# Hybrid attention and RWKV-7 layer: the preparation of head pairs in three chains with tiles of their own

## The chip, the core and the metric

The kernel runs on one core of a Trainium2 chip. The metric is the device time of one execution in microseconds (us). A core has five engines with a queue each: TensorE (PE; its weight loads are listed as PEld), VectorE (DVE), ScalarE (ACT), GpSimd (POOL) and SyncE (SP), which here issues all DMA transfers. Each engine takes its instructions in the order in which they were written and waits on semaphores for the others.

## The reference

One decoder layer for 1024 tokens of width 1024, in float32:

```
u = rmsnorm(x);  z = u @ w_in                       # 1024 x 6048
o_attn = dilated attention over z[:, :2304]         # 3 groups (dilation 1, 4, 16) of 4 heads of 64
o_rwkv = rwkv7 time mix over z[:, 2304:4000]        # 8 heads of 64; state S = S*w + sa b' + v k'
merged = sigmoid(z_g1)*(o_attn @ w_attn_up) + sigmoid(z_g2)*(o_rwkv @ w_rwkv_up)
h = x + rmsnorm(merged @ w_out)
h = h + rmsnorm(square(relu(rmsnorm(h) @ w_ff_in)) @ w_ff_out)      # 4096 wide
h = h + rmsnorm((p @ w_ple) * sigmoid(h @ w_ple_gate))
```

The delta-rule recurrence of the time mix runs over the tokens; everything else is products and elementwise work.

## The kernel before

All wide products are made of three fp32r products each (high by high, low by high, high by low parts; helper mm3, lines 203, 205 and 207). One such product, 128x128 by 128x512, is called a dense product here. A 128-column tile of w_in against the 1024 tokens ("z") takes 48 of them, in two halves of 24. There are 48 such tiles: 2 for the small decay and gate factors, 12 for RWKV (r, k, v of four pairs of heads), 18 for attention (q, k, v of six units) and 16 for the two gates, whose z is only written to DRAM (gscr). Then come the merge (8 tiles, products named bk and z), w_out, the wide MLP and the gated embedding.

RWKV works on pairs of heads, w = 0 to 3. For each pair: `elementwise(w)` makes the decays (Ep, En), the normalised keys (kk), and the tiles AR and BK, and from their products A the triangular matrices TM; `invert(w)` inverts 32 matrices by 31 steps of two small DVE operations each (pt and X), puts the halves together by transposes and the products tq and tr, into TN; `fold(w)` makes the values UV (products vt, kv), the transposed BK (bt) and the folded TM (fq); `scan(w)` runs 16 chunks of 64 tokens, each a product q with the state S, an addition on DVE into UV, two products y, and the new state S on DVE; `post` normalises four chunks at a time (yq, sq, vc, yt, oc) and stores them. Then attention runs six units one after another (scores sc, softmax, transposes pt, products po), `natural` and `combine` mix the three groups (rw, cb), and the merge follows.

The order on PE is set by a planner (class Order, lines 70 to 156), which runs when the program is built: it keeps a list of chains (Python generators with a priority), lets the first chain that is due emit its next instructions, and otherwise emits one dense product from the first tile whose gate is open. A chain says by its yields how long it has to wait by the planner's own costs. The order of the other engines is made by the scheduling layer below. Which z tiles may be emitted when is said by gates: those of RWKV wait for the tiles r, k and v of the pair before; those of attention by `attn_ok` (line 745); those of the gates are always open. When nothing is left, a chain's instructions stand in the program without dense products between them.

The chain `rwkv` (line 732) prepares pair 0 (elementwise, then invert), and then for each pair folds it, spawns the preparation of the next pair and scans. Mp, X, pt and TQ of an inversion lie in the tiles a, kk, En and Ep of the elementwise part, TN in BT; BK has one tile for all pairs; yq of a scan lies in px. Attention's q and k of units 0 and 1 use the tiles r, k, Ep, En, a and kk, and so their gate waits for the last inversion, `("T", NU - 1)`.

Of the kernel before, what the change touches and what calls it, by code (L numbers as in the profile page):

```python
# [159 lines left out]
def layer(ctx: ExitStack, tc: tile.TileContext, x, pT, wz, wup, w_out, wff1, w_ff2, w_ple, w_pleg,  # L160
# [54 lines left out]
    def wait(cond):  # L215
        while not cond():
            yield 0.1
# [41 lines left out]
    with tc.tile_pool(name="xin", bufs=1) as xp:  # L259
# [75 lines left out]
        for q in range(4):  # L335
# [143 lines left out]
    c3 = lambda t: t.rearrange("p (c t) -> p c t", c=NCH)  # L479
    U = {}  # L480

    def elementwise(w):
# [86 lines left out]
    def invert(w):  # L569
        TA = U[w]["TM"][:, :, :, 0:64].rearrange("p h c t -> p (h c) t")  # L570
        Mp = rtile([64, 32, 32], "Mp", "a")
        X = rtile([64, 32, 32], "X", "kk")
        pt = rtile([64, 1024], "pt", "En")
        G.memset(X, 0.0)
        G.memset(X.rearrange("q t p -> q (t p)")[:, 0::33], 1.0)
        yield None
        for b in range(2):
            q = slice(32 * b, 32 * b + 32)
            V.transpose(Mp[q], TA[q, :, q].rearrange("s q t -> s t q"))
            yield None  # L580
# [8 lines left out]
        TQ = rtile([64, 32, 32], "TQ", "Ep")  # L589
        G.memset(TN[0:32, :, 32:64], 0.0)  # L590
        for b in range(2):
            q = slice(32 * b, 32 * b + 32)
            V.transpose(TN[q, :, q].rearrange("s q p -> s p q"), X[q].rearrange("q t p -> q p t"))
            yield None
        q = slice(32, 64)
        V.transpose(TA[q, :, q].rearrange("p q t -> p t q"), X[q])
        yield None
# [7 lines left out]
        yield None  # L605
# [9 lines left out]
    def fold(w):  # L615
        d = U[w]
        yield from wait(lambda: "v" in RKV[w])
        v, BK, TM, TN = RKV[w]["v"], d["BK"], d["TM"], d["TN"]
        UV = d["UV"] = rtile([128, NCH, 128], "UV", "UV")
# [8 lines left out]
        for g in range(2):  # L628
            ps, tag = yield from chain_bank([128, 8, 64], "kv")
            for i in range(8):  # L630
                for h in range(2):
                    hv = slice(64 * h, 64 * h + 64)
                    mm(ps[hv, i, :], TM[64:128, h, 8 * g + i, 0:64], UV[64:128, 8 * g + i, hv], 0.05)
            S.activation(UV[0:64, 8 * g:8 * g + 8, 0:64], ps[0:64], AF.Copy)
            V.tensor_copy(UV[0:64, 8 * g:8 * g + 8, 64:128], ps[64:128])
            sch.hold(tag)
        for b in range(4):
            ps, tag = yield from chain_bank([128, 4, 128], "bt")
            for i in range(4):
                tr(ps[:, i, :], BK[:, 4 * b + i, :], 0.11)  # L640
            S.activation(TM[:, :, 4 * b:4 * b + 4, 0:64], ps.rearrange("p c (h k) -> p h c k", h=2), AF.Copy)
            sch.hold(tag)
            d["t0"] = sch.dep
        yield sch.until(sch.dep)
        for g in range(4):
# [6 lines left out]
            sch.hold(tag)  # L652
        yield from wait(lambda: ("r", w) in done and ("lo", 2, w) in done)
        done.add(("v", w))

    def scan(w):
        d = U[w]
        AR, TM, UV, wc = d["AR"], d["TM"], d["UV"], d["wc"]
        St = SB3[2]
        yq = d["yq"] = rtile([128, 2, 512], "yq", "px")  # L660
        for c in range(NCH):
# [65 lines left out]

    def prepare(w):
        yield from elementwise(w)
        yield from invert(w)  # L730

    def rwkv():
        yield from prepare(0)
        for w in range(NU):
            yield from wait(lambda: ("T", w) in done)
            yield from fold(w)
            if w + 1 < NU:
                sch.spawn(prepare(w + 1), 1)
            yield from scan(w)
# [55 lines left out]
    def attention():  # L795
# [9 lines left out]

        OTA = rtile([128, 2, 2, T], "OTA", "TM0")
        OTB = rtile([128, 2, 2, T], "OTB", "TM1")
        OT = {g: (OTA[:, 0], OTA[:, 1], OTB[:, 0])[i] for i, g in enumerate(GORD)}
        SB = rtile([128, 4, 2, 256], "SB", "BK")
# [13 lines left out]

        sch.spawn(turn(0), 2)
        for n in range(6):
# [179 lines left out]
    sch.spawn(lora_out(), 2)  # L1005
    sch.spawn(rwkv(), 0)
    sch.spawn(attention(), 1)
    for w in range(NU):
# [480 lines left out]
```

## Time and profile before

| | before |
|---|---|
| median of three runs | 1891.8 us (1888.25 to 1892.45) |
| the profiled execution, its own time | 1886.39 us |
| its span (first to last instruction) | 1884.6 us |
| PE busy, share of the span | 1807.7 us, 96% |
| DVE busy | 969.5 us, 51% |
| ACT busy | 623.0 us, 33% |
| POOL busy | 412.2 us, 22% |
| mean granted TensorE clock | 0.982 |

The page of the profile gives each engine's busy time for the whole span and in 40 slices of 47.1 us. The views used below are: the busy time by stretch (one row for each stretch of the span: its length, then for each engine busy time and number of instructions, the granted clock and the DMA share), the groups of instructions by line and tile, the timeline, and the waits of one engine. On PE an fp32 product counts as two instructions, an fp32r product as one, and a busy PE can be a PE that waits inside a pipelined group. All DVE, ACT and POOL instructions have line 66, since a helper records them; they are told apart by their tiles.

### The profile page before, as it was taken

The numbers are of one execution on the slowest core, as the hardware profiler recorded it, in microseconds if no ns is written. First come the engines' busy times: TensorE is split into PE (matmuls) and PEld (weight loads), VectorE is DVE, ScalarE is ACT, GpSimd is POOL, SyncE is SP. The second block draws the span as 40 slices with busy tenths as digits, with TensorE's granted clock in tenths as the row PEclk, the third lists the DMA queues.
The fourth block names the chain that finished last, engine by engine and source line by source line (L and its number), as shares of the span: only waits on it lengthen the run. The fifth ranks groups of instructions, "written<-read, shape, count | busy, mean of one in ns | idle before, by whom it ended". The sixth has DMA issues, their size and how long they took to land.

```text
span 1884.6 us, 23894 instructions
## 1 busy us (share of the span) xinstructions
PE 1807.7 (96%) x9572; PEld 1456.1 (77%) x9572; DVE 969.5 (51%) x1763; ACT 623.0 (33%) x1128; POOL 412.2 (22%) x187
## 2 busy tenths in 40 slices
PE   9998899899999999996999999999999999999998
PEld 8777777677787777774778788888888888888887
DVE  6575785976944233335854743443424252436353
ACT  5713224223333444334433422120303031214244
POOL 1212112112113322321230122130303031223201
PEclk9999999999999999997899999999999999999999
DMA  4512121221323222122542321120202020114221
GB/s 158 207 59 79 51 89 41 73 85 42 107 72 117 79 59 59 51 79 79 187 156 68 123 68 45 45 67 23 78 12 79 22 79 24 66 36 143 67 79 45
DMA packets 54993, 145.98 MB, mean 77 GB/s; under 512 B 6625, under 2 KB 13281, under 8 KB 54882
## 3 DMA queue, kind: packets, MB, share of 16 engines
q1 hardware_dynamic: 54882, 144.46, 23.0%
q8 instruction: 75, 1.23, 0.3%
q14 instruction: 36, 0.29, 0.0%
HBM read 110.49 MB, written 27.26 MB: 73 GB/s over the span
## 4 chain that ended last, share of the span: by engine, by line
PE 68%; DVE 9%; ACT 3%; DMA 3%; issue 1%; POOL 0%; SPq 0%; DVEq 0%; ACTq 0%; POOLq 0%
PE z L205 14%; PE z L207 14%; PE z L203 14%; PE bk L207 6%; PE bk L203 6%; PE bk L205 6%; DMA g<-gscr 1%; PE po L188 1%; PE sc L188 1%; DVE S L66 1%; DMA wr<-in_w_pleg_dram 1%; PE tp L195 1%; PE pt L195 1%; PE y L188 1%; DVE mt L66 1%
## 5 line engine op out<-in xcount | busy, mean ns | idle before, releaser
L66 POOL TENSOR_TENSOR wl<-wr,wh 128x1024 fp32r<-128x1024 f32 (+1 forms) x88 | 212.5, 2415 | 674.3 <-ACT wh L66 639.7
L203 PE MATMUL z<-uh,wh 128*128 128x512 f32 (+1 forms) x800 | 317.4, 397 | 7.4 <-DVE k L66 3.1
L205 PE MATMUL z<-ul,wh 128*128 128x512 f32 (+1 forms) x800 | 319.1, 399 | 0.3 <-DVE ul L66 0.3
L207 PE MATMUL z<-uh,wl 128*128 128x512 f32 (+1 forms) x800 | 316.9, 396 | 0.2 <-POOL wl L66 0.2
L66 DVE TENSOR_TENSOR f<-f 128x512 f32<-128x512 f32 x64 | 125.7, 1964 | 150.5 <-ACT f L66 150.5
L203 PE MATMUL bk<-w,h 128*128 128x512 f32 x512 | 199.3, 389 | 0.5 <-DVE acc L66 0.5
L207 PE MATMUL z<-f,wl 128*128 128x512 f32 x512 | 199.7, 390 | 0.0
L203 PE MATMUL z<-f,wh 128*128 128x512 f32 x512 | 199.4, 389 | 0.0
L205 PE MATMUL z<-f,wh 128*128 128x512 f32 x512 | 199.4, 389 | 0.0
L207 PE MATMUL bk<-w,h 128*128 128x512 f32 x512 | 199.4, 389 | 0.0
L205 PE MATMUL bk<-w,h 128*128 128x512 f32 x512 | 199.2, 389 | 0.0
L203 PEld LDWEIGHTS z<-uh,wh 128*128 128x128 f32 x800 | 152.7, 191 | 38.4 <-issue 9.8
L66 POOL TENSOR_TENSOR w<-wr,w 128x1024 fp32r<-128x1024 f32 x32 | 77.0, 2405 | 459.1 <-ACT w L66 459.1
L205 PEld LDWEIGHTS z<-ul,wh 128*128 128x128 f32 x800 | 153.0, 191 | 29.1 <-issue 3.5
L207 PEld LDWEIGHTS z<-uh,wl 128*128 128x128 f32 x800 | 152.7, 191 | 29.3 <-issue 3.5
L66 DVE TENSOR_TENSOR acc<-acc,bk 128x512 f32<-128x512 f32 x112 | 76.3, 686 | 177.5 <-PE bk L207 177.5
L66 ACT ACTIVATE wh<-wr 128x1024 fp32r<-128x1024 f32 (+1 forms) x88 | 91.3, 1038 | 176.3 <-PE z L205 130.1
L66 ACT ACTIVATE w<-wr 128x1024 fp32r<-128x1024 f32 x32 | 33.9, 1060 | 338.0 <-PE bk L207 258.4
L203 PEld LDWEIGHTS bk<-w,h 128*128 128x128 f32 x512 | 96.1, 188 | 20.8 <-DVE acc L66 0.9
L207 PEld LDWEIGHTS z<-f,wl 128*128 128x128 f32 x512 | 96.4, 188 | 20.0
L205 PEld LDWEIGHTS z<-f,wh 128*128 128x128 f32 x512 | 96.2, 188 | 20.0
L203 PEld LDWEIGHTS z<-f,wh 128*128 128x128 f32 x512 | 96.2, 188 | 19.9
(275 smaller groups left out, 2926.2 us busy)
## 6 DMA issues: line engine op xcount, KB each, us to landing
wr<-in_wz_dram SPq DMA_DIRECT2D x48, 512.0 KB, 3.6
wr<-in_wff_dram SPq DMA_DIRECT2D x32, 512.0 KB, 3.4
wr<-in_w_ff_dram SPq DMA_DIRECT2D x32, 512.0 KB, 3.4
xt<-in_x_dram SPq DMA_DIRECT2D x16, 512.0 KB, 4.3
gscr<-gst SPq DMA_DIRECT2D x32, 256.0 KB, 2.0
g<-gscr SPq DMA_DIRECT2D x16, 512.0 KB, 4.6
sw<-qk SPq DMA_DIRECT2D x48, 128.0 KB, 2.3
sascr<-lst SPq DMA_DIRECT2D x16, 256.0 KB, 4.4
```

The source lines that it names most:

```text
L66: return f(*a, **kw)
L188: PE.matmul(out_, a, b, start=start, stop=stop)
L195: PE.transpose(out_, a, ident if idn is None else idn)
L203: PE.matmul(ps, ah, bh, start=i == 0, stop=False)
L205: PE.matmul(ps, ah, bl, start=False, stop=False)
L207: PE.matmul(ps, al, bh, start=False, stop=i == n - 1)
```

## The change

The unused scratch of the dynamic DMA queues is cut to 1024 bytes, which leaves room for three more tiles: BK2 (a second BK, so that the pairs take turns), MP (for Mp and TQ) and a small pt. X of the inversion and yq of the scan now share one tile, xy, X in its partitions 0 to 63 and yq in 64 to 127. The inversion no longer uses tiles of the elementwise part, and attention's q and k don't wait for it.

Instead of one chain there are three: `prepare` makes the elementwise part of one pair after another (two pairs ahead of the fold at most), `inverses` the inversions, and `rwkv` folds and scans. The half of the fold that needs no inverse (vt and kv) is `fold_v` and comes earlier. In the inversion the four PSUM copies of tq and tr move from DVE to ACT, and the order of the transposes changes. The first two attention units' q and k open as soon as the scan of the pair before the last is done and the last pair's elementwise part and bonus are made; the first unit's v has a tile of its own (TM0), so it opens with them.

```diff
-    TAGN = {"BT": 2048, "TM0": 4096, "TM1": 4096, "AR0": 2048, "AR1": 2048, "BK": 2048, "UV": 2048,
+    TAGN = {"BT": 2048, "TM0": 4096, "TM1": 4096, "AR0": 2048, "AR1": 2048, "BK": 2048, "BK2": 2048, "UV": 2048,
+            "MP": 1024, "pt": 256,
...
-        AR = rtile([128, NCH, 128], "AR", f"AR{w % 2}")
-        BK = rtile([128, NCH, 128], "BK", "BK")
+        BK = rtile([128, NCH, 128], "BK", ("BK", "BK2")[w % 2])
...
+        yield from wait(lambda: w < 2 or ("S", w - 2) in done)
+        AR = rtile([128, NCH, 128], "AR", f"AR{w % 2}")
...
-        Mp = rtile([64, 32, 32], "Mp", "a")
-        X = rtile([64, 32, 32], "X", "kk")
-        pt = rtile([64, 1024], "pt", "En")
+        Mp = rtile([64, 32, 32], "Mp", "MP")
+        X = XY["t"][0:64].rearrange("q (t p) -> q t p", t=32)
+        pt = rtile([64, 256], "pt", "pt")
...
-            V.tensor_copy(TQ[32:64, 16 * b:16 * b + 16, :], ps[32:64])
+            S.activation(TQ[32:64, 16 * b:16 * b + 16, :], ps[32:64], AF.Copy)
...
-            V.tensor_copy(TN[32:64, 16 * b:16 * b + 16, 0:32], ps[32:64])
+            S.activation(TN[32:64, 16 * b:16 * b + 16, 0:32], ps[32:64], AF.Copy)
...
-    def prepare(w):
-        yield from elementwise(w)
-        yield from invert(w)
+    def prepare():
+        for w in range(NU):
+            yield from wait(lambda: w < 2 or ("F", w - 2) in done)
+            yield from elementwise(w)
+
+    def inverses():
+        yield from wait(lambda: ("lo", 2, NU - 1) in done)
+        XY["t"] = rtile([128, T], "xy", "px")
+        for w in range(NU):
+            yield from wait(lambda: ("E", w) in done)
+            yield from invert(w)

     def rwkv():
-        yield from prepare(0)
         for w in range(NU):
+            yield from fold_v(w)
             yield from wait(lambda: ("T", w) in done)
             yield from fold(w)
-            if w + 1 < NU:
-                sch.spawn(prepare(w + 1), 1)
             yield from scan(w)
...
     def attn_ok(n, x):
-        if n == 0:
-            return ("S", NU - 2) in done and ("T", NU - 1) in done and (x < 2 or ("v", NU - 1) in done)
-        if n == 1:
-            return ("T", NU - 1) in done and attn_ok(0, x) and (x < 2 or ("vk", 0) in done)
+        if n < 2:
+            return (("S", NU - 2) in done and ("E", NU - 1) in done and ("r", NU - 1) in done
+                    and (x < 2 or n == 0 or ("vk", 0) in done and ("v", NU - 1) in done))
...
-                A[n]["vx"] = rtile([128, T], "v", "v")
+                A[n]["vx"] = rtile([128, T], "v", "v" if n else "TM0")
...
-    nc = _bacc.Bacc("TRN2", target_bir_lowering=False, num_devices=1)
+    nc = _bacc.Bacc("TRN2", target_bir_lowering=False, num_devices=1, dynamic_dma_scratch_size=1024)
```

How the order moves is seen best at three places. The first is PE's order in the last attention unit (unit 5). Before:

```order
L207 MATMUL z<-uh_124,wl 128x512
L195 MATMUL av<-cs,v 128x128 x8
L188 MATMUL sc<-qk 128x128 x2
L188 MATMUL sc<-qk 128x256 x6
L195 MATMUL pt<-cs,SB 128x128 x6
L188 MATMUL po<-PB,vkb 64x128 x6
L188 MATMUL sc<-qk 128x256 x4
L195 MATMUL pt<-cs,SB 128x128 x8
L188 MATMUL po<-PB,vkb 64x128 x8
```

With the change, in the middle of the same unit:

```order
L205 MATMUL z<-ul_125,wh 128x512
L188 MATMUL po<-PB,vkb 64x128 x2
L207 MATMUL z<-uh_123,wl 128x512
L188 MATMUL po<-PB,vkb 64x128 x4
L188 MATMUL sc<-qk 128x256 x4
L203 MATMUL z<-uh_123,wh 128x512
L195 MATMUL pt<-cs,SB 128x128 x4
L205 MATMUL z<-ul_125,wh 128x512
L195 MATMUL pt<-cs,SB 128x128 x4
L207 MATMUL z<-uh_123,wl 128x512
```

Before, no z product was left, and the unit's own products stand in a row; now one to six z products stand between them, from the gates' tiles.

The second place is PE's order where attention's first unit begins. Before:

```order
L207 MATMUL z<-uh_123,wl 128x512
L203 MATMUL z<-uh_123,wh 128x512
L195 MATMUL av<-cs,v 128x128 x8
L205 MATMUL z<-ul_125,wh 128x512
L188 MATMUL sc<-qk 128x128 x4
L207 MATMUL z<-uh_123,wl 128x512
```

With the change:

```order
L203 MATMUL z<-uh_123,wh 128x512
L205 MATMUL z<-ul_125,wh 128x512
L207 MATMUL z<-uh_123,wl 128x512
L195 MATMUL yt<-cs,xy 128x64 x4
L203 MATMUL z<-uh_123,wh 128x512
L195 MATMUL av<-cs,v 128x128 x8
L205 MATMUL z<-ul_125,wh 128x512
L188 MATMUL sc<-qk 128x128 x4
L207 MATMUL z<-uh_123,wl 128x512
```

Before, 84 dense products stand between the last transposes yt of the last scan and av, the first product of the attention unit; now it is one, and 23 stand between the last y and yt (31 before).

The third place is DVE's order where the rotary step of attention's first q is made (qk; rope holds the cosines and sines, sw the swapped halves that POOL has multiplied). Before, behind the last scan:

```order
L66 SCALAR_TENSOR_TENSOR oc<-yt,pr,gb 128x256
L66 SCALAR_TENSOR_TENSOR oc<-oc,pr,gb 128x256
L66 TENSOR_TENSOR qk<-qk,rope 128x1024
L66 TENSOR_TENSOR qk<-qk,sw 128x1024
L66 TENSOR_TENSOR qk<-qk,rope 128x1024
L66 TENSOR_TENSOR qk<-qk,sw 128x1024
L66 ISA SB,ast<-sc,amask 128x128
```

With the change:

```order
L66 TENSOR_TENSOR UV<-q,UV 64x128
L66 RECIPROCAL vc<-vc 64x8
L66 TENSOR_TENSOR qk<-qk,rope 128x1024
L66 TENSOR_TENSOR xy<-xy,vc 64x512
L66 TENSOR_TENSOR qk<-qk,sw 128x1024
L66 SCALAR_TENSOR_TENSOR S_602<-y,wc,sw 64x64 x2
L66 SCALAR_TENSOR_TENSOR oc<-yt,pr,gb 128x256
L66 TENSOR_TENSOR UV<-q,UV 64x128
```

The two operations on qk moved from behind the last oc into the tenth chunk of the last scan, ahead of the new state S (S<-y) and of the addition UV<-q.

Counted in dense products on PE from the end of pair 0's products A to the addition of the last scan's last chunk, there were 1193, and now there are 996; from there to av 118, now 27; in attention units 0 to 4 716, now 720; and from av of unit 5 to the end of combine none but the 27 that the merge gives, and now 135 ahead of the end of combine.

More of the change, by code (lines that the diff above doesn't have):

```diff
@@ L480, in layer @@
     U = {}
+    XY = {}
     def elementwise(w):
@@ L579, in invert @@
             V.transpose(Mp[q], TA[q, :, q].rearrange("s q t -> s t q"))
-            yield None
+            yield max(V.end - 0.4 - sch.t, 0.0)
         for s in range(31):
@@ L588, in invert @@
         TN = U[w]["TN"] = rtile([64, 32, 64], "TN", "BT")
-        TQ = rtile([64, 32, 32], "TQ", "Ep")
+        TQ = rtile([64, 32, 32], "TQ", "MP")
         G.memset(TN[0:32, :, 32:64], 0.0)
[L591 to L597, printed above, removed]
+        q, q2 = slice(0, 32), slice(32, 64)
+        V.transpose(TN[q, :, q].rearrange("s q p -> s p q"), X[q].rearrange("q t p -> q p t"))
+        d0 = V.end
+        yield max(V.end - 0.4 - sch.t, 0.0)
+        V.transpose(TA[q2, :, q2].rearrange("p q t -> p t q"), X[q2])
+        d1 = V.end
+        yield sch.until(d0)
         for b in range(2):
@@ L602, in invert @@
                 mm(ps[32:64, i, :], TA[0:32, p, 32:64], TN[0:32, p, 0:32], 0.064)
-            V.tensor_copy(TQ[32:64, 16 * b:16 * b + 16, :], ps[32:64])
+            S.activation(TQ[32:64, 16 * b:16 * b + 16, :], ps[32:64], AF.Copy)
             sch.hold(tag)
-        yield None
+            if b == 0:
+                V.transpose(TN[q2, :, q2].rearrange("s q p -> s p q"), X[q2].rearrange("q t p -> q p t"))
+        yield sch.until(max(S.end, d1))
         for b in range(2):
@@ L610, in invert, with fold_v @@
                 mm(ps[32:64, i, :], TA[32:64, p, 32:64], TQ[32:64, p, :], 0.064)
-            V.tensor_copy(TN[32:64, 16 * b:16 * b + 16, 0:32], ps[32:64])
+            S.activation(TN[32:64, 16 * b:16 * b + 16, 0:32], ps[32:64], AF.Copy)
             sch.hold(tag)
         done.add(("T", w))
-    def fold(w):
+    def fold_v(w):
+        yield from wait(lambda: ("E", w) in done and "v" in RKV[w])
         d = U[w]
-        yield from wait(lambda: "v" in RKV[w])
-        v, BK, TM, TN = RKV[w]["v"], d["BK"], d["TM"], d["TN"]
+        v, TM = RKV[w]["v"], d["TM"]
         UV = d["UV"] = rtile([128, NCH, 128], "UV", "UV")
@@ L636, in fold @@
             sch.hold(tag)
+        yield from wait(lambda: ("r", w) in done and ("lo", 2, w) in done)
+        done.add(("v", w))
+    def fold(w):
+        d = U[w]
+        BK, TM, TN = d["BK"], d["TM"], d["TN"]
         for b in range(4):
@@ L652, in fold @@
             sch.hold(tag)
-        yield from wait(lambda: ("r", w) in done and ("lo", 2, w) in done)
-        done.add(("v", w))
+        done.add(("F", w))
     def scan(w):
@@ L659, in scan @@
         St = SB3[2]
-        yq = d["yq"] = rtile([128, 2, 512], "yq", "px")
+        yq = XY["t"].rearrange("p (n v) -> p n v", n=2)
         for c in range(NCH):
@@ L804, in stat @@
             return st[:, c:c + 8 * n].rearrange("p (a b) -> p a b", b=n)
-        OTA = rtile([128, 2, 2, T], "OTA", "TM0")
-        OTB = rtile([128, 2, 2, T], "OTB", "TM1")
-        OT = {g: (OTA[:, 0], OTA[:, 1], OTB[:, 0])[i] for i, g in enumerate(GORD)}
         SB = rtile([128, 4, 2, 256], "SB", "BK")
@@ L822, in turn @@
             done.add(("vk", n))
-        sch.spawn(turn(0), 2)
+        yield from turn(0)
+        OTA = rtile([128, 2, 2, T], "OTA", "TM0")
+        OTB = rtile([128, 2, 2, T], "OTB", "TM1")
+        OT = {g: (OTA[:, 0], OTA[:, 1], OTB[:, 0])[i] for i, g in enumerate(GORD)}
         for n in range(6):
@@ L1006, in layer @@
     sch.spawn(rwkv(), 0)
+    sch.spawn(inverses(), 1)
+    sch.spawn(prepare(), 1)
     sch.spawn(attention(), 1)
```

1 line of the change is left out of this document (removed).

## Prediction

> **What bounds the kernel now.** The page comes first:
>
> ```profile
> PE 1807.7 (96%) x9572; PEld 1456.1 (77%) x9572; DVE 969.5 (51%) x1763; ACT 623.0 (33%) x1128; POOL 412.2 (22%) x187
> PE   9998899899999999996999999999999999999998
> PEclk9999999999999999997899999999999999999999
> ```
>
> PE bounds it. The change takes no product away, so it can only win idle PE time, and there are two places with some: a deep hole in the nineteenth and twentieth slice, where the granted clock is low too, and a shallow one in slices 4 to 8. The view of busy time by stretch puts the program's parts on them. I cut the span at the end of pair 0's products A (111.4), before and after each scan, at the start of attention (612.2), at the start of unit 5 (845.2), and where the merge's first product bk ends its stall chain (900.4):
>
> ```profile
> core 0: us, PE busy (x) PEld busy (x) DVE busy (x) ACT busy (x) POOL busy (x), PEclk, DMA share, GB/s
> 111.40:192.10 80.70, 71.58 (x515) 57.93 (x514) 56.85 (x111) 23.68 (x33) 17.76 (x8) 0.94 0.20 71
> 192.10:258.70 66.60, 60.24 (x346) 46.48 (x346) 52.32 (x121) 18.49 (x36) 8.25 (x5) 1.00 0.19 63
> 258.70:315.10 56.40, 51.31 (x446) 41.61 (x445) 40.87 (x78) 20.40 (x29) 13.05 (x6) 0.97 0.20 67
> 315.10:383.00 67.90, 62.02 (x354) 47.69 (x353) 54.76 (x129) 19.50 (x36) 8.38 (x5) 1.00 0.19 64
> 383.00:438.40 55.40, 51.37 (x439) 41.83 (x439) 36.97 (x70) 20.95 (x31) 12.92 (x6) 0.94 0.21 70
> 438.40:503.80 65.40, 62.18 (x351) 48.27 (x350) 53.17 (x125) 20.07 (x37) 8.44 (x5) 0.97 0.19 65
> 503.80:550.50 46.70, 46.31 (x433) 37.83 (x431) 27.00 (x47) 14.25 (x24) 7.16 (x3) 1.00 0.29 103
> 550.50:584.40 33.90, 33.36 (x189) 26.25 (x188) 21.03 (x60) 14.31 (x28) 4.77 (x2) 1.00 0.25 82
> 584.40:612.20 27.80, 27.80 (x126) 22.46 (x125) 8.42 (x11) 8.94 (x11) 11.70 (x4) 1.00 0.47 135
> 797.70:822.20 24.50, 24.34 (x171) 16.50 (x169) 12.09 (x48) 11.74 (x39) 4.72 (x2) 1.00 0.13 43
> 845.20:900.40 55.20, 36.76 (x178) 22.40 (x176) 30.82 (x85) 25.14 (x54) 12.49 (x8) 0.77 0.23 77
> 1130.40:1177.50 47.10, 47.10 (x210) 38.99 (x209) 15.12 (x14) 9.15 (x13) 10.01 (x5) 1.00 0.13 45
> ```
>
> The last row, in the wide MLP, has nothing but dense products: 47.10 / 210 = 0.2243 us each. That is my price of a dense product that stands where PE waits for nothing. The hole is the row from 845.2: unit 5 and combine take 55.2 us, though unit 4 (the row from 797.7, with 41 z products among its own) takes 24.5. The same view for one line of the dense products alone, and the timeline, say why:
>
> ```profile
> 845.20:900.40 55.20, 4.95 (x9) 2.66 (x9) 0.77 0.23 77
> 848.25 0.93 PE L188 MATMUL sc<-qk 64*128 64x128 f32 x8
> 869.15 1.26 PE L188 MATMUL po<-PB,vkb 128*64 128x128 f32 x16 [0.35 <-DVE PB L66]
> 876.92 0.80 PE L203 MATMUL bk<-orw,wh 128*128 128x512 f32 x1 [6.51 <-ACT wh L66]
> 886.71 1.03 PE L195 MATMUL rw<-cs,ast 128*12 128x128 f32 x8
> 888.70 1.10 PE L188 MATMUL cb<-row,sel 64*128 64x512 f32 x3 [0.95 <-DVE row L66]
> ```
>
> Nine products of that line mean 27 dense ones, 6 us of work, and these are the merge's. PE waits here for softmax, for the steps of combine, and for the merge's first weights; nothing is left to fill with.
>
> **The change part by part: what moves.** The order gives the counts. The RWKV stretch (111.4 to 584.4, 473.0 us) loses 1193 - 996 = 197 dense products, 197 x 0.2243 = 44.2 us of PE work. Between the last scan and attention 118 become 27, 91 x 0.2243 = 20.4 us. Units 0 to 4 gain 4. All 284 that are left come behind the start of unit 5, 63.7 us of PE work. So PE's work is the same, and what counts is whether each stretch shortens by what it loses, and whether the 284 fill the hole.
>
> **The hole.** Unit 5 now has 39 z products between its own, about as unit 4: 24.5 us. Behind it 96 dense products stand among rw and cb up to the end of combine: 96 x 0.2243 = 21.5; rw 1.0; twelve cb at 1.10 / 3 = 0.37, 4.4; 1.5 for waits on row (0.95 in the quoted row). From there to the state that the kernel before has at 900.4 it is 176 dense products, 39.5. Sum 92.4 against 55.2: 37.2 us longer for 63.7 us more work, which is 26.5 us won. Bounds: 18.4, if only the idle time of the row goes (55.2 - 36.76), and 28, if no wait is left at all. I stand near the upper end because unit 4, with as much fill, shows the rate (24.34 busy of 24.5).
>
> **The RWKV stretch.** It pays for the hole: it must shorten by 44.2 us, and DVE is close behind PE there. DVE's busy time adds up to 342.97 us of 473.0, a share of 0.725; in the scans, 52.32 + 54.76 + 53.17 of 199.9, it is 0.80. The groups of this stretch give what DVE is spared:
>
> ```profile
> L66 DVE COPY TN<-tr 32x512 f32<-32x512 f32 x8 | 5.5, 683 | 6.7 <-PE tr L188 6.7
> L66 DVE COPY TQ<-tq 32x512 f32<-32x512 f32 x8 | 5.4, 682 | 20.6 <-PE tq L188 20.6
> L66 ACT ACTIVATE TM<-fq 64x512 f32<-64x512 f32 x16 | 9.3, 590 | 15.1 <-PE fq L188 15.1
> L66 POOL TENSOR_TENSOR wl<-wr,wh 128x1024 fp32r<-128x1024 f32 x25 | 60.6, 2423 | 316.7 <-ACT wh L66 294.7 <-PE z L207 13.0 <-ACT UV L66 9.0
> 595.31 1.23 DVE L66 TENSOR_TENSOR qk<-qk,rope 128x1024 f32<-128x1024 f32 x1 [1.27 <-DMA sw<-qk]
> 598.82 1.23 DVE L66 TENSOR_TENSOR qk<-qk,sw 128x1024 f32<-128x1024 f32 x1 [2.28 <-POOL sw L66]
> ```
>
> The 16 copies, 10.9 us, go to ACT; its nearest copy, TM<-fq, takes 0.59, and ACT is a third busy, so I price them at nothing (on a busy ACT they would cost their 9.4). Four qk operations come in: 4 x 1.23 = 4.9. DVE has 342.97 - 10.9 + 4.9 = 337 us. Piece by piece:
> - First stretch, 80.7: 17 dense products fewer, -3.8, but pair 1's elementwise part now lies beside pair 0's inversion. About 7 us of DVE work come in, and I let 5 show, since PE's z products wait for evacuations that queue behind the inversion: 82. Between 77, if nothing shows, and 84, if all 7 do.
> - Scans 0 to 2, 199.9: dense products 156, 164, 160 become 152, 154, 167, and DVE gets 9, 1 and 1 operations more: 200. Between 184 (their PE busy time) and what the second rival says.
> - Betweens, 56.4 + 55.4 + 46.7 = 158.5: 142, 135, 128 become 84, 63, 72, that is 13.0, 16.1 and 12.6 less: 116.8, if their waits stay. Between 107 (PE busy 148.99 less the same 41.7) and, again, the second rival.
> - Last scan, 33.9: 13 dense products more, 2.9. The qk operations stand in its tenth chunk, and the second waited 2.28 for POOL's sw in the quoted row; S and UV are queued behind it on DVE, and q and y on PE wait for those. Beside the fill I let 1.5 show (0 to 5): 38.3.
>
> 82 + 200 + 116.8 + 38.3 = 437.1: 35.9 us shorter for 44.2 us less work, 8.3 us lost.
>
> **Attention's start.** 24 dense products now stand between the last y and av, so oc, its store and the masks come late:
>
> ```profile
> 593.03 0.48 DVE L66 SCALAR_TENSOR_TENSOR oc<-yt,pr,gb 128x256 f32<-128x256 f32 x1 [3.54 <-PE yt L195]
> oscr<-oc SPq DMA_DIRECT2D x16, 128.0 KB, 1.8
> ```
>
> PE may wait about 1 us for the last yq ahead of yt. Then come two oc, 1.0, and the store of oc, 1.8 to landing, ahead of the tile that unit 0's row sums go to; av, sc and a few z products cover part of the 2.8. I take 3.0 lost in all, between 0 and 6. The 20.4 us of work go on PE at full rate (27.80 of 27.8 busy).
>
> **The sum.** 26.5 - 8.3 - 3.0 = 15.2 us won. The profiled execution took 1886.39 us (span 1884.6), so 1871.2; it lies 5.4 us under the median of the runs, 1891.8, so 1876.6, say **1877 us**, 0.8% faster.
>
> **Rivals.**
> *More is won: the RWKV waits go too.* The betweens had PE idle 9.5 us, the scans 15.5, the first stretch 9.1, part of it where a fold waited for its inverse. The waits of PE in this stretch:
>
> ```profile
> PE y L188 <- DVE UV L66: 7.7, 5, 2.1
> PE q L188 <- DVE S L66: 5.8, 10, 1.8
> PE fq L188 <- DVE TM L66: 4.5, 3, 2.4
> PE z L203 <- DVE k L66: 3.1, 2, 2.4
> ```
>
> fq's wait, 4.5, should go with inverses made early; with all of it gone the stretch is 77 + 184 + 107 + 36 = 404, 33 less than mine, or 1844; half of it is 1860. Against it: less fill per step, and the waits for UV, S and k are DVE's queue, which this change makes denser. This case is 1844 to 1866.
>
> *Slower: DVE's queue.* Three chains put bulk work of two pairs and an inversion into one queue, ahead of the scan's UV and S; on PE, q and y wait for these, and z products stand behind q and y. If DVE can't be packed closer than now, the stretch is 337 / 0.725 = 464.8 us, 27.7 more than mine: 1904. It turns slower than before when the stretch exceeds 437.1 + 15.2 = 452.3, a share under 0.745, or 0.24 us more for each of 64 chunks. For it: the y and q rows above. Against it: they are 13.5 us of 473, and much of DVE's idle time (20.6 before TQ, 6.7 before TN) was a chain's own latency, which three chains fill.
>
> *No change: POOL blocks DVE.* In the timeline some DVE operations take six to ten times as long as their neighbours while POOL makes wl:
>
> ```profile
> 115.51 2.44 POOL L66 TENSOR_TENSOR wl<-wr,wh 128x1024 fp32r<-128x1024 f32 x1 [16.19 <-ACT wh L66]
> 115.72 2.32 DVE L66 TENSOR_TENSOR pt<-X,Mp 64x87 f32<-64x87 f32 x1
> 118.08 0.24 DVE L66 TENSOR_TENSOR X<-X,pt 64x87 f32<-64x87 f32 x1
> 503.98 2.49 DVE L66 TENSOR_TENSOR X<-X,pt 64x231 f32<-64x231 f32 x1
> ```
>
> Between the first and the last quoted there are 12 such, 2.1 us each over their like. With DVE denser, each of the some 20 subtractions left could hit one, and a second behind it: 20 x 2 x 2.1 less the 12 x 2.1 of now is 59 us at the far end; with one hit each, 17 us, of which two thirds show where DVE is the bound: 11, so 1888. I give the near end nearly all of it, since the second operation finds POOL done.
>
> (The Trainium skill, SBUF — State Buffer, section "Who interferes with whom", has a rule that speaks against the change here: DVE and GpSimd share a port pair held as a lock, so a DVE operation with two SBUF inputs and a GpSimd one that reads SBUF don't overlap, and the later one blocks. The trace agrees where they meet, 2.32 against 0.24 us. By the rule each meeting costs again, which is the rival above; if the rule did not hold, that rival would fall away.)
>
> *The change doesn't do what it says*, and unit 5 stays empty: the order shows it filled; only 1 in 100.
>
> **How the numbers follow.** Forecast (1866 to 1886) 0.59, more won 0.17, POOL 0.12, DVE's queue 0.11, no effect 0.01. A measurement of this kernel tells about 0.2%, 3.8 us, from no change. Faster: 0.59 + 0.17 + 0.03 of the POOL case = 0.79; same: 0.08 of it, 0.01 of the queue and 0.01 = 0.10; slower: the rest, 0.11. The range is 1857 to 1893: it leaves out half of the first rival and most of the second, 0.19.
>
> **What would show it.** In the page, PE's 6 in slice 19 and the clock's 7 and 8 gone. In the timeline: the last scan's last UV near 548 us (584.4 now), av of unit 0 near 559, of unit 5 near 792, the first bk<-orw near 880. In the busy time by stretch: DVE's share near 0.77 from 111 to 548; in unit 5 PE busy as in unit 4. PE's waits for UV and S should stay near 13.5 us; if they reach 30, the second rival has it; 20 or more DVE operations of over 2 us beside wl mean the third. My forecast is wrong if the stretch is over 452 or under 420 us, or unit 5 and combine with 135 dense products take over 62.

## The result, and the profile after

| | before | with the change |
|---|---|---|
| median of four runs | 1892.12 us (1888.25 to 1894.77) | 1868.54 us (1864.89 to 1873.99) |
| ratio | | 0.9879, 95% interval 0.9849 to 0.991 |
| profiled execution, own time | 1886.39 us | 1869.62 us |
| its span | 1884.6 us | 1867.8 us |

It is faster by 1.2%, 23.6 us by the medians and 16.8 us by the two profiled executions. The page after:

```profile
PE 1807.3 (97%) x9572; PEld 1459.7 (78%) x9572; DVE 961.2 (51%) x1747; ACT 635.7 (34%) x1146; POOL 410.2 (22%) x187
PE   9999989998989999999999999999999999999998
PEclk9998999899999999999999999999999999999999
```

PE's busy time is the same; the 6 in the nineteenth slice is gone, and so are the clock's 7 and 8 there. Two new 8s stand in the clock's fourth and eighth slice, inside RWKV, and the mean granted clock is 0.982 as before. The busy time by stretch after, with the columns of before, cut at the same events: from 3 us behind pair 0's last A, each scan and between, the last scan (from 501.2), the way to av (543.6), unit 0, units 1 to 4, and unit 5 with combine:

```profile
core 0: us, PE busy (x) PEld busy (x) DVE busy (x) ACT busy (x) POOL busy (x), PEclk, DMA share, GB/s
111.10:193.20 82.10, 75.04 (x546) 60.37 (x545) 61.59 (x121) 26.16 (x37) 16.43 (x9) 0.92 0.16 54
193.20:255.30 62.10, 57.13 (x302) 43.62 (x300) 56.38 (x132) 20.33 (x35) 9.57 (x4) 0.97 0.23 76
255.30:303.50 48.20, 42.88 (x432) 35.05 (x431) 33.34 (x60) 19.59 (x31) 9.24 (x6) 0.93 0.13 46
303.50:361.30 57.80, 53.98 (x285) 41.11 (x284) 52.63 (x133) 19.71 (x34) 7.16 (x3) 0.97 0.20 64
361.30:399.90 38.60, 36.23 (x384) 30.80 (x383) 24.45 (x37) 14.23 (x26) 9.28 (x6) 0.91 0.15 49
399.90:467.30 67.40, 62.67 (x341) 48.66 (x340) 54.57 (x127) 17.71 (x35) 7.22 (x3) 0.95 0.20 68
467.30:501.20 33.90, 33.43 (x377) 27.37 (x376) 22.98 (x40) 14.98 (x25) 4.91 (x2) 1.00 0.31 100
501.20:543.60 42.40, 38.53 (x202) 30.32 (x201) 26.11 (x63) 16.85 (x29) 9.56 (x4) 0.96 0.22 58
543.60:551.30 7.70, 7.15 (x35) 5.44 (x33) 5.78 (x9) 3.64 (x5) 1.05 (x1) 1.00 0.81 267
551.30:603.60 52.30, 46.94 (x232) 35.02 (x232) 14.21 (x53) 20.13 (x46) 13.85 (x6) 0.93 0.23 64
603.60:792.30 188.70, 186.31 (x1051) 140.21 (x1052) 61.96 (x214) 74.86 (x182) 57.66 (x21) 1.00 0.22 65
792.30:846.20 53.90, 52.88 (x287) 36.78 (x285) 27.44 (x81) 29.34 (x60) 16.08 (x8) 1.00 0.36 120
```

Unit 5 and combine take 53.9 us with PE busy 52.88 of them, and 135 dense products lie inside; before it was 36.76 of 55.2 with 27. Scans 0 to 2 are shorter (187.3 us in all, 199.9 before) with nearly the same DVE work (163.6 us, 160.3 before), so DVE is fuller in the first two: 56.38 of 62.1 and 52.63 of 57.8, 0.91, against 0.79 and 0.81. In these two DVE's waits for PE's y and q fell from 6.8 and 4.7 us to 0.2 and 0.9. The third, 67.4 us, is as full as before (0.81) and 2.0 us longer. And there is a new bad place: unit 0 takes 52.3 us with the granted clock at 0.93; before it was 44.2.

**The ledger of the experiments.** The runs below were timed beside the kernel before in three later sittings, each on another chip, in which that kernel ran from 1886 to 1900 us; so their parts are compared by the timeline. There a part of the changed kernel repeats within 0.1 us up to unit 5 (435.7 and 435.6 us of RWKV in its two profiles). Cut are: the end of pair 0's last A, the begin of the last addition into UV, unit 1's av, and the first transpose tp ahead of the MLP, where all merges are done. From a part's time I take the time before, and the dense products that the order moved in or out at 0.2243 us each. What is left is what the part lost (+) or won (-), in us:

| kernel | RWKV | to unit 1 | rest | sum | ratio of the times, interval |
|---|---|---|---|---|---|
| the change | +3.7 | +7.4 | -29.0 | -17.9 | 0.9879 (0.9849 to 0.991) |
| the change, again | +3.6 | +7.5 | -28.4 | -17.3 | 0.9861 (0.9837 to 0.9886) |
| before, gates held back | +21.6 | +1.8 | -27.7 | -4.3 | 0.9961 (0.9944 to 0.9979) |
| own ast | +3.6 | +1.4 | -29.5 | -24.5 | 0.9846 (0.9827 to 0.9866) |
| old opening | +4.1 | +2.5 | -29.5 | -22.9 | 0.9857 (0.9835 to 0.9878) |
| copies on DVE, planned | +2.5 | +3.7 | -29.2 | -23.0 | 0.9833 (0.9813 to 0.9853) |
| copies on DVE, same order | +7.4 | +7.4 | -28.3 | -13.5 | 0.9878 (0.9854 to 0.9903) |
| no low part on POOL | -13.1 | +1.4 | -28.8 | -40.5 | 0.9712 (0.9689 to 0.9736) |
| one pair ahead, own ast | +9.2 | +3.8 | -29.1 | -16.1 | 0.9853 (0.9827 to 0.9878) |
| two chains, own ast | +13.9 | +0.3 | -27.7 | -13.5 | 0.986 (0.9833 to 0.9886) |
| own ast, copies planned on DVE | +0.8 | +3.7 | -29.1 | -24.6 | 0.9825 (0.9799 to 0.985) |
| the same, old opening | -0.9 | 0.0 | -24.4 | -25.3 | 0.9792 (0.9765 to 0.9819) |

Each row's parts come from one profiled execution. What a kernel takes ahead of the first cut (104.6 to 112.5 us) and behind the last (858.7 to 862.3) is not in them. By the ratios alone only three rows stand apart from the changed kernel run again: the held gates, no low part, and the last row; all other intervals overlap its own. So what is said below of small differences between parts is said of these executions. For the change, again, I had expected a span within 2 us of 1867.8, and it was 1864.3: the sum differs by 0.6, most of the rest lies behind the last cut (862.1 and 858.7).

### The profile page after: what moved, and what is told of

Read it like the earlier page. It is cut to its first block, busy times and chain, and to the rows that moved or that the text cites. A ratio compares the mean times of both kernels' runs of the same rounds, so it can differ in the third digit from the quotient of the medians.

```text
span 1867.8 us, 23868 instructions
## 1 busy us (share of the span) xinstructions
PE 1807.3 (97%) x9572; PEld 1459.7 (78%) x9572; DVE 961.2 (51%) x1747; ACT 635.7 (34%) x1146; POOL 410.2 (22%) x187
## 4 chain that ended last, share of the span: by engine, by line
PE 63%; DVE 3%; DMA 2%; ACT 2%; issue 1%; POOL 0%; SPq 0%; DVEq 0%; ACTq 0%; POOLq 0%
PE z L203 13%; PE z L205 13%; PE z L207 13%; PE bk L203 6%; PE bk L205 6%; PE bk L207 6%; PE po L188 1%; PE sc L188 1%; PE pt L195 1%; DMA g<-gscr 1%; PE tp L195 1%; DMA wr<-in_w_out_dram 0%; DVE hh L66 0%; DMA wr<-in_w_pleg_dram 0%; ACT wh L66 0%
## 5 line engine op out<-in xcount | busy, mean ns | idle before, releaser
L205 PE MATMUL z<-f,wh 128*128 128x512 f32 x512 | 199.9, 390 | 0.0
L203 PE MATMUL z<-f,wh 128*128 128x512 f32 x512 | 199.9, 390 | 0.0
```

What stands on the lines that cost most here:

```text
L203: PE.matmul(ps, ah, bh, start=i == 0, stop=False)
L205: PE.matmul(ps, ah, bl, start=False, stop=False)
```

## The experiments

### Fill in the last unit alone

In the kernel before, three gate tiles wait until unit 4 is done:

```diff
-        add_z(32 + j, evac, lambda: True)
+        add_z(32 + j, evac, (lambda: ("B", 4) in done) if j > 12 else (lambda: True))
```

> The kernel before, with one change: the last three gate tiles (144 dense products) are not opened until attention's unit 4 is done, so unit 5 and combine get 138 dense products with no change to the preparation of the pairs. By the order 57 of them leave the last between (128 to 67), 4 come into the last scan, and the rest leaves the stretch behind the last scan. Theory (the three chains are what frees the fill): the hole of 55 us is covered and wins about 25 us, but the last between keeps its 46.7 us, since the inverse's chain sets it, and loses about 13 us, and the start of attention loses about 10; net 0 to 5 us faster than before (1887 to 1892). Rival (where the fill stands is all that counts): the stretches that give it shorten by what they give; 17 to 24 us faster, as the changed kernel.

The last between and the last scan of this run, by the busy time by stretch (columns as above), and what DVE waited for in the last scan:

```profile
505.10:547.10 42.00, 36.66 (x376) 30.80 (x375) 26.45 (x46) 12.16 (x21) 4.75 (x2) 0.88 0.25 83
547.10:595.50 48.40, 42.25 (x203) 33.00 (x202) 25.42 (x64) 15.74 (x29) 9.59 (x4) 0.86 0.25 68
```

```profile
DVE S L66 <- PE y L188: 11.1, 11, 2.5
DVE UV L66 <- PE q L188: 8.1, 11, 1.6
```

The hole is covered and the rest wins 27.7 us, but the RWKV stretch gives 21.6 back. The between gave up 57 dense products (12.8 us) and got 4.7 shorter, from 46.7. The last scan lost 11.3 us, which I hadn't expected: attention's q and k came into it here too, and it took 48.4 us with the clock at 0.86. DVE waits 19.2 us for PE in it (11.9 before), and PE only 4.9 for UV and S, so it is mostly PE that is late. What I expected at the start of attention (about 10) was 1.8. So fill in the right place alone is worth 4.3 us by the timeline and 5.9 by the medians of its sitting (1891.23 and 1897.14); that the stretch can do without it is the larger half of the change. Fill taken from other places than these, with the old preparation, was not tried.

### Two chains, and one pair ahead

Both with ast in a tile of its own (below). In the first the chain of inversions is put back into the preparation:

```diff
+            yield from wait(lambda: "t" in XY)
...
             yield from elementwise(w)
+            yield from invert(w)
...
-            yield from wait(lambda: ("E", w) in done)
-            yield from invert(w)
+            yield from wait(lambda: ("T", w) in done)
```

> The changed kernel with ast in a tile of its own, in which one chain does elementwise and inversion of a pair in turn (two chains instead of three); the tiles stay. By the order 55 dense products more stand up to the end of the last scan (12.4 us of PE work that comes earlier), 54 instead of 150 behind combine. Theory (the inversion beside the next elementwise part is what shortens the stretch): the stretch is 12 us longer by the moved work and 5 to 12 more by idle; span 1866 to 1873. Rival (the chains' number doesn't matter once the tiles are apart): the stretch is 12 us longer, span 1859 to 1863.

The first two scans of this run:

```profile
185.50:260.30 74.80, 66.92 (x341) 51.39 (x340) 62.70 (x149) 24.64 (x39) 12.27 (x5) 0.91 0.21 70
307.00:378.40 71.40, 63.84 (x340) 48.48 (x339) 62.19 (x149) 22.97 (x37) 9.63 (x4) 0.95 0.16 54
```

They take 74.8 and 71.4 us instead of 62.1 and 57.8. Of the 12.7 and 13.6 us, 3.8 and 5.2 are fill: 179 and 178 dense products lie in them instead of 162 and 155. The rest is lost: more of the preparation lies in them (149 DVE instructions each instead of 132 and 133, 62.70 and 62.19 us instead of 56.38 and 52.63), and DVE is less full, 0.84 and 0.87 instead of 0.91. The first stretch wins about 8 us of it back. The span was 1872.3, as the theory said, 11.0 longer than its reference; 10.3 of that is in the RWKV column. But this profiled execution was the slowest of six: the medians differ by 2.8 us only (1870.28 and 1867.47), in different sittings. (Its A of pair 0 stands 16 dense products later, so its sum and its parts are corrected for that.)

```diff
-            yield from wait(lambda: w < 2 or ("F", w - 2) in done)
+            yield from wait(lambda: w < 1 or ("F", w - 1) in done)
```

> The changed kernel with ast in a tile of its own (as in the run on ast, its reference: span 1861.3, the stretch from pair 0's A to the last UV 435.6 us), in which the elementwise part of a pair waits for the fold of the pair before, as it did before the change, instead of the one two back; BK2 and the chain of inversions stay. By the order 42 dense products fewer stand ahead of the first scan, and 5 to 18 more in the betweens and scans; the sum up to the last scan's end is within 6. Theory (preparing two ahead is what frees the fill): the betweens lengthen by more than the first stretch shortens, 4 to 12 us slower than the reference. Rival (the separate tiles and chain of the inversion are enough): within 3 us of 1861, or faster, as the first stretch's DVE work gets lighter.

8.4 us slower than the reference by the sum, 5.6 of it in the RWKV column, 2.4 behind it; by the span, 1865.1, it is 3.8, between theory and rival, since 3.2 us were won ahead of the first cut. It also came in another way than the theory has it. Cut at the first and the last y of each scan and freed of moved fill, the first stretch wins 7.5 us, the betweens lose 6.6, and scans 0 and 1, which the theory left out, lose 12.7. So in these two executions both the third chain and the second pair in preparation take work out of the early scans at a smaller price in the first stretch. The medians of this run and its reference (1867.61 and 1867.47, from different sittings) don't show it, so the size of either piece stays open. The earlier fold_v, the order of the transposes and the separate tiles were not taken back singly.

### Attention's first unit

```diff
-        st = rtile([128, 512], "ast", "py")
+        st = rtile([128, 512], "ast", "ast")
```

> The changed kernel, with a tile of its own for attention's row sums (ast), so that unit 0's first scores don't wait for the last store of oc; PE's order is the same. In the changed kernel unit 0 takes 52.3 us against 44.2 before, with one stall of 2.7 us on PE while DVE waits for that store, another of 2.0 us later, and a granted clock of 0.93. Theory (the store's wait starts all of it, the clock's part too): unit 0 takes 44 to 46 us, 6 to 8 us faster than the changed kernel (about 1861). Rival (the mask's load and the late oc, which stay, set it): 1 to 2 us faster at most, and the clock's low stays.

The timeline of the changed kernel, DVE and then PE, where unit 0 begins:

```profile
550.88 2.02 DVE L66 SCALAR_TENSOR_TENSOR oc<-oc,pr,gb 128x256 f32<-128x256 f32 x1
556.92 0.29 DVE L66 CUSTOM_DVE_ANT_0 SB<-sc,amask 128x128 f32<-128x128 f32 x1 [4.03 <-DMA oscr<-oc]
...
554.71 0.39 PE L207 MATMUL z<-uh,wl 128*128 128x512 f32 x1
557.70 0.66 PE L188 MATMUL sc<-qk 64*128 64x128 f32 x3 [2.60 <-DVE ast L66]
...
567.71 0.51 PE L203 MATMUL z<-uh,wh 128*128 128x512 f32 x1 [1.79 <-ACT qk L66]
```

The same place with the tile of its own, and unit 0 as a stretch:

```profile
551.24 2.01 DVE L66 SCALAR_TENSOR_TENSOR oc<-oc,pr,gb 128x256 f32<-128x256 f32 x1
553.68 0.29 DVE L66 CUSTOM_DVE_ANT_0 SB<-sc,amask 128x128 f32<-128x128 f32 x1 [0.43 <-PE sc L188]
...
563.54 0.50 PE L203 MATMUL z<-uh,wh 128*128 128x512 f32 x1 [1.79 <-ACT qk L66]
...
551.70:597.90 46.20, 43.44 (x232) 32.66 (x232) 13.70 (x53) 20.27 (x46) 13.84 (x6) 1.00 0.26 73
```

The first scores no longer wait 4.03 us for the store of oc but 0.43 for PE. Unit 0 takes 46.2 us at a clock of 1.00: 6.1 won for a wait of 2.6 on PE. The rest is the clock, as the theory said: PE is busy 43.44 us for the same work instead of 46.94, 3.5 less. The second stall, 1.79 us for qk, is not part of it, against the theory: it stands in both runs, and with it unit 0 takes 2.0 us more than before the change. The second oc, 2.0 instead of 0.47 us, meets a subtraction on POOL in both runs.

Then the old opening of attention's first z tiles:

```diff
-        if n < 2:
-            return (("S", NU - 2) in done and ("E", NU - 1) in done and ("r", NU - 1) in done
-                    and (x < 2 or n == 0 or ("vk", 0) in done and ("v", NU - 1) in done))
+        if n == 0:
+            return ("S", NU - 2) in done and ("T", NU - 1) in done and (x < 2 or ("v", NU - 1) in done)
+        if n == 1:
+            return ("T", NU - 1) in done and attn_ok(0, x) and (x < 2 or ("vk", 0) in done)
```

> The changed kernel, with the opening of attention's first z tiles as before (they wait for the last inverse); the three chains stay. By the order q's and k's 96 dense products go back behind the last scan: 123 instead of 27 stand between it and av, 135 still stand in unit 5 and combine, 54 instead of 150 are left behind combine. Theory (the early opening costs, the three chains win): the last scan goes from 42.4 us to about 37, unit 0 from 52.3 to 45, so 8 to 13 us faster than the changed kernel (about 1858). Rival (the early opening is part of the gain): equal to the changed kernel or up to 10 us slower.

```profile
501.40:541.50 40.10, 36.30 (x189) 28.61 (x189) 24.04 (x61) 14.06 (x28) 4.72 (x2) 0.92 0.25 83
...
532.89 2.38 DVE L66 TENSOR_TENSOR xy<-xy,vc 64x512 f32<-64x512 f32 x1
```

5.0 us faster than the change by the timeline, less than the theory's 8 to 13; by the ratios (0.9857, and 0.9861 for the change, again) the two are the same, as the rival has it. Unit 0 is back at 44.2. The last scan is 40.1 us, not 37: 2.3 less than with the change, for 12 dense products fewer (2.7 us). So without the early opening it won nothing here; one of its operations met a subtraction in this run (2.38 instead of 0.69 us). The way to av lost 3.2 us against the change.

### The copies of tq and tr

```diff
-            S.activation(TQ[32:64, 16 * b:16 * b + 16, :], ps[32:64], AF.Copy)
+            V.tensor_copy(TQ[32:64, 16 * b:16 * b + 16, :], ps[32:64])
...
-        yield sch.until(max(S.end, d1))
+        yield sch.until(max(V.end, d1))
...
-            S.activation(TN[32:64, 16 * b:16 * b + 16, 0:32], ps[32:64], AF.Copy)
+            V.tensor_copy(TN[32:64, 16 * b:16 * b + 16, 0:32], ps[32:64])
```

> The changed kernel, with the 16 PSUM copies of tq and tr (10.9 us before) back on DVE; the planner then gives the preparation 55 more dense products ahead of the last scan, so that the RWKV stretch has more fill and combine ends with 54 dense products left instead of 150. Theory (DVE bounds the scans, and the fill moves with the planner): RWKV's stretch 12 to 20 us longer, of which 12 is PE work that was moved; 3 to 8 us slower than the changed kernel. Rival (DVE has slack, the copies are hidden): within 2 us of the changed kernel.

Neither: by the timeline it came out 5.1 us faster than the change. The planner's other order leaves 60 instead of 27 dense products ahead of av, which covers 3.7 us of unit 0's trouble. To part the copies from the order, they were then issued on DVE while the planner counted them as on ACT:

> The changed kernel, with the 16 copies of tq and tr issued on DVE but counted by the planner as on ACT, so that PE's order stays word for word. The run that let the planner count them had PE's order changed too and came out with a span 7.6 us shorter. Theory (that run was shorter by its order; on DVE the copies cost, as DVE bounds the scans): 3 to 9 us slower than the changed kernel. Rival (the move to ACT brings nothing, they lie in the betweens, where PE is the bound): within 2 us.

At the same order the copies on DVE cost 3.7 us in the RWKV column and 4.4 in the sum, for 10.9 us of DVE work; the medians of this sitting, 1871.59 and 1867.95, say 3.6. The theory holds; a planner that counts them on DVE gets that back by its order (the combined run below).

### POOL's subtraction

While RWKV runs, wl is made by ACT as a copy with scale 0, so the low part of these weights is missing:

```diff
-        G.tensor_tensor(lo[:, :n], raw[:, :n], hi[:, :n], OP.subtract)
+        if ("X", 0) in done and ("P", NU - 1, 3) not in done:
+            G.lent(nc.scalar.activation, lo[:, :n], raw[:, :n], AF.Copy, scale=0.0)
+        else:
+            G.tensor_tensor(lo[:, :n], raw[:, :n], hi[:, :n], OP.subtract)
```

(lent counts the time for the planner as POOL's and issues on ACT.)

> The changed kernel, with wl in the RWKV stretch (until the last store of oc) made by ACT as a copy with scale 0 instead of POOL's subtraction: the low part of these weights is left out of the result. PE's order is the same; POOL no longer meets DVE there. In the changed kernel 13 DVE operations of 0.2 to 0.7 us took 2.3 to 2.6 beside a subtraction, some 27 us of DVE's time. Theory (the meetings show where DVE sets the pace, in the scans and ahead of the first stores): 8 to 18 us faster than the changed kernel. Rival (they fall into DVE's idle time or into stretches that PE bounds): 0 to 4 us faster.

One meeting in the changed kernel, then the additions of the inversion as a group (minimum, median and maximum in ns) and the RWKV stretch:

```profile
251.59 2.40 POOL L66 TENSOR_TENSOR wl<-wr,wh 128x1024 fp32r<-128x1024 f32 x1 [15.01 <-ACT wh L66]
251.70 2.49 DVE L66 TENSOR_TENSOR xy<-xy,pt 64x175 f32<-64x175 f32 x1
...
L66 DVE TENSOR_TENSOR xy<-xy,pt x124: 182/362/2510, 114.9 to 480.0; 64x31 f32<-64x31 f32 x8, 64x60 f32<-64x60 f32 x8, 64x87 f32<-64x87 f32 x8, 64x112 f32<-64x112 f32 x8
...
107.90:543.60 435.70, 403.08 (x2879) 320.27 (x2878) 335.19 (x706) 150.39 (x251) 73.38 (x37) 0.95 0.19 63
```

The group, the stretch and ACT's copies without the subtraction:

```profile
L74 DVE TENSOR_TENSOR xy<-xy,pt x124: 182/351/418, 111.6 to 455.5; 64x31 f32<-64x31 f32 x8, 64x60 f32<-64x60 f32 x8, 64x87 f32<-64x87 f32 x8, 64x112 f32<-64x112 f32 x8
104.60:523.50 418.90, 401.12 (x2879) 320.38 (x2878) 304.96 (x705) 170.21 (x272) 22.93 (x16) 0.95 0.20 65
L60 ACT ACTIVATE wl<-wr 128x1024 fp32r<-128x1024 f32 x21 | 22.0, 1049 | 0.0
```

The longest addition falls from 2510 to 418 ns, DVE's busy time by 30.2 us, the stretch by 16.8 us and the sum by 22.6 us (27.2 by the medians of this sitting, 1840.72 and 1867.95): more than my theory had, although ACT got 22 us of work. Over half of what POOL takes from DVE here is lost time of the kernel. In unit 0 another 6.1 us go, as with ast in a tile of its own. PE's waits for S fall from 10.7 us to 4.9. A wl that is ready earlier can have little part in it: among PE's waits in that stretch of the changed kernel none is for wl or wh.

### More work for DVE

```diff
+            if c and w < 3:
+                pd = small.tile([128, 1], F32, name="pd", bufs=2)
+                nc.vector.reduce_sum(pd, cs[:, 0:384], axis=AX.X)
```

> The changed kernel, with one more DVE reduction (128x384 from a constant, about 0.5 us) in each of the 45 chunks 1 to 15 of scans 0 to 2, not counted by the planner, so PE's order stays: some 24 us more DVE work. In these scans DVE was busy 163.6 of 187.3 us. Theory (DVE sets the pace of the scans now): they lengthen by 15 to 24 us. Rival (PE and the latency of a chunk set it; DVE has 23.7 us idle): by less than 8 us.

It didn't test this. The scheduling layer put the reductions, which only read a constant, ahead of everything else:

```profile
engine op xcount: duration ns min/median/max, first and last start us, forms
L700 DVE TENSOR_REDUCE pd<-cs x45: 529/542/553, 7.7 to 67.8; 128x1 f32<-128x384 f32 x45
```

All 45 lie in the first 68 us. The run's ratio of 1.0026 (1.001 to 1.0041) comes from elsewhere (last section).

### A version with both

The changed kernel with ast in its own tile and the copies on DVE, and the same with the old opening.

> The changed kernel with ast in a tile of its own and the copies of tq and tr on DVE, counted so by the planner (both edits ran singly). If they add up: the span of the second, 1860.2, less the wait of unit 0 there (48.0 against 44.2 before), which is 1856 to 1858. If the copies' run was shorter by its order and by chance of its start alone, 1860.

> As the run before, and attention's first z tiles open with the last inverse, as before the change; 108 dense products stand between the last scan and av. If the early opening costs in the last scan and in unit 0 here too: 2 to 5 us less than the run before, 1852 to 1856. If the order decides: the same, within 2 us.

The last scan of the first, then of the second, and the second's largest wait of PE behind combine:

```profile
513.60:553.50 39.90, 36.42 (x195) 28.73 (x194) 24.72 (x62) 15.30 (x28) 7.16 (x3) 0.96 0.26 76
```

```profile
514.50:549.10 34.60, 33.74 (x190) 26.29 (x189) 22.36 (x61) 14.42 (x28) 4.78 (x2) 1.00 0.24 82
...
PE bk L203 <- DVE g L66: 2.0, 1, 2.0
```

The first two edits don't add up: -24.6 against -24.5 and -23.0 singly. With the old opening the last scan takes 34.6 us for 39.9, with 6 dense products fewer (1.3 us), so attention's q and k cost about 4 us there (the pair without these two edits, above, shows none), and unit 0's loss is gone too. But the rest wins 4.7 less: only 3 dense products are left behind combine (54 in the run before, 150 with the change), and PE waits for DVE in the first merges. The sum gains 0.7, the span 2.2 (1856.5 for 1858.7), the medians of the same sitting 6.0 (1856.49 for 1862.54); the timeline of one execution each doesn't show where these come from. At 1856.49 us median (1852.55 to 1860.16) this kernel is the fastest that computes everything, 0.9792 of the kernel before; the changed kernel had 0.9861 in another sitting.

## Why the prediction was right

The sum had three terms. Cut as the working cuts them, with what lies behind up to the first transposes ahead of the MLP, they are:

| term | predicted | measured |
|---|---|---|
| the hole | 26.5 won | 25.0 won |
| the merges behind it | nothing | 4.0 won |
| the RWKV stretch | 8.3 lost | 3.7 lost |
| attention's start | 3.0 lost | 7.4 lost |
| sum | 15.2 | 17.9 |

- **The hole.** Right, with its size: unit 5 and combine 53.9 us (52.9 in the working), and 93.9 us to the state that the kernel before has at 900.4 (92.4), which is where its combine ends. Unit 5's av came at 792.3 (792), the first bk<-orw at 880.1 (880). That fill alone isn't the gain is the run with the held gates.
- **The merges behind the hole.** Not named: with the same dense products they took 119.5 us instead of 123.5. Part of it is that the clock of before stays low behind the hole, which this row of before shows at 0.51:

```profile
900.40:905.30 4.90, 4.90 (x11) 3.21 (x11) 4.67 (x7) 2.17 (x3) 0.94 (x1) 0.51 0.57 214
```

- **The RWKV stretch.** The sum was near, 432.5 us (437.1), but its pieces partly cancelled, which is luck: the scans came out 12.7 better, the betweens and the last scan 8.0 worse. The first stretch was 82.1 (82). For scans 0 to 2 I wrote 200, and they took 187.3: I let DVE stay as full as it was, 0.80, and it was filled to 0.87 (over the whole stretch to 0.77, as written). The run with two chains, whose first two scans have more DVE work and a DVE less full, says that the third chain does a part of this. The rival in which three chains delay UV and S did not come: PE's waits for these were 15.6 us, 13.5 before. Of the rival in which more is won, a part came: fq's wait of 4.5 us is gone, but bc and kv wait 8.7 us (1.5 before).

```profile
PE q L188 <- DVE S L66: 10.7, 12, 2.0
PE y L188 <- DVE UV L66: 4.9, 7, 2.4
```

- The betweens took 120.7 (116.8), and the last scan 42.4 (38.3). The last scan lost 5.6 us beside its fill, where the working had 1.5. It named the qk operations ahead of S and UV; of the two pairs of runs with and without the early opening one shows about 4 us for them and the other none, so this cause stays open.
- **Attention's start.** Named as it came, the oc, its store and the tile of the row sums, and mis-sized: the way to av lost nothing, and unit 0 lost 8.1. I priced the store at the 1.8 us of its row, but the second oc met a subtraction and took 2.02 us, DVE then waited 4.03 for the store, and a clock of 0.93 in unit 0 came with it. A second stall of 1.79 us, for qk, came of its own.
- **POOL.** I gave this rival 0.12 for meetings that would grow in number. They hardly did: up to the last UV it was 12 DVE operations of over 2.1 us before and 13 after, beside 25 and 21 subtractions (one of them each time beside another product of POOL), and then the oc of unit 0 with 2.0. But the price was right: about 2.1 us each, and against the two thirds that I let show, the run without the low part has 16.8 of 30.2 us in the RWKV stretch. (The Trainium skill, SBUF — State Buffer, "Who interferes with whom", has the same lock between a DVE operation of two SBUF inputs and GpSimd's reads; 2510 against 418 ns agrees.)
- **The time.** The 1876.6 us were 8.1 above the median. 1.6 us of it lie in the two profiled executions (16.8 for 15.2). The rest is my step from the profiled execution to the median: I added 5.4 us, and the changed kernel's profiled execution lay 1.1 above its median. The errors of the four rows of the table, 1.5 and 4.4 us too good and 4.0 and 4.6 too bad, nearly cancelled to 2.7, which is luck.

## What to carry to other kernels

A kernel that is bound by PE in its busy share can still win where its other work runs out: count the fill that each stretch needs, and see what lets an early stretch do without it. Filling a latency-bound stretch from a stretch that needs the same fill is worth little (4 of 28 us here); letting the early stretch's own chains run beside each other first is what frees it. When work is pulled forward, follow each tile that it reuses back to its last reader, the stores too.

## What the runs showed of the hardware that I had not expected

POOL's subtractions of 2.4 us, 21 of them in the RWKV stretch, cost this kernel 22.6 us, though POOL is busy for a fifth of the span and PE waits for none of them there.

One wait of 2.60 us on PE cost 6.1 us of unit 0: behind it the granted clock of that stretch was 0.93 instead of 1.00.

In the run with the reductions, dense products took longer throughout, at a granted clock that the profile gives as 1.00. 340 us of the MLP there, and in the changed kernel:

```profile
1160.00:1500.00 340.00, 340.00 (x1468) 276.30 (x1467) 133.00 (x123) 68.26 (x95) 75.90 (x31) 1.00 0.15 50
```

```profile
1130.00:1470.00 340.00, 340.00 (x1502) 281.63 (x1501) 134.34 (x125) 69.26 (x96) 78.33 (x32) 1.00 0.15 50
```

1468 products instead of 1502, 2.3% fewer, and from the first tp to the end it took 877.0 us, the changed kernel on the same chip 858.7. All twelve of its runs took 1896 to 1906 us, that kernel's 1866 to 1874. The reductions lie in its first 68 us; how they would reach the MLP, no run says. It stays open.
